# Neighbourhood attention: key columns in storage order for the scores, and a bias table with the row offset inside each block of key columns

## The chip, the cores and the metric

The kernel runs on one core of one Trainium2 chip. The metric is the device time of one execution in microseconds; a kernel's time is the median over its runs. The profile is one execution taken by the hardware profiler. Engines are named as the profile names them: PE (TensorE matmuls), PEld (TensorE weight loads, which overlap PE), DVE (VectorE), ACT (ScalarE), POOL (GpSimd) and SP (SyncE, whose queue issues nearly all DMAs).

## The reference

A trunk of two layers over 1024 tokens of width 1024. Each layer is a token mixer and a squared-ReLU MLP of width 4096, each with a pre-RMSNorm and a residual add; a last RMSNorm closes it. The mixer of the first layer is the neighbourhood attention that the change touches, that of the second a gated DeltaNet.

The tokens form a grid of 16 rows and 64 columns. In the attention each of 16 heads of width 64 lets a query see 8 rows and 16 columns of keys around it, with a learned bias per head, row offset and column offset:

```
s = einsum('bhrd,bhkd->bhrk', q, k) * scale + bias     # bias from rpb[h, drow, dcol]
p = softmax(where(mask, s, -inf))                      # mask: 8 rows x 16 columns around the query
o = p @ v;   out = (o reshaped) @ w_o
```

Everything is float32.

## The kernel before

Each large product is made of three passes in a reduced float format (F32R): every operand is split into a high and a low part, and hi x hi, hi x lo and lo x hi are added up in PSUM. Weights come by DMA in pieces of 256 KB (`wraw`, three buffers, line 97), ACT makes the high part (line 108) and DVE the low part (line 109), and `product` (line 120) runs the matmuls at line 132.

Tokens are kept in the order (column block of 8, row, column inside the block). So one tile of 128 tokens is one block of 8 grid columns with all its 16 rows, there are 8 such tiles, and a query tile needs the keys of its own block and of the blocks beside it: three key tiles (384 keys), or two (256) for the first and the last.

`load_x` (line 312) loads and transposes x and computes the values v for all heads; its second half of the columns uses four late weight loads (`wvraw`, line 320). `na` (line 403) then goes through 8 pairs of heads, n = 0 to 7. For each pair it computes k and q with `product`, splits them, and copies halves between partitions with DMAs from POOL's queue (lines 440 and 447). Then for each query tile t and each of the two heads:

- two score matmuls (line 468): q against the keys of two or three tiles, first hi x hi over 64 rows, then both cross products at once over 128 rows. The moving operand `kv` is a view of the keys with the row outermost: row, block, column. It is read in runs of 8 elements, and the scores lie in PSUM in the order (row, block, column);
- DVE (line 471) adds the bias, negates, and takes the extreme over the keys in the same instruction;
- ACT (line 474) takes the exponential and its sum. It reads and writes through the same permuting view, so that the result `e` lies in the order (block, row, column) of the keys as they are stored;
- DVE divides by the sum (lines 478 and 479), PE transposes 128 keys at a time (line 482), ACT or DVE copies the result (lines 485 and 487), and PE multiplies by v (line 492).

The bias comes from a table in DRAM, `natab` [head, query column, row offset, 56 key columns]. The 56 key columns are three sets: 24 for inner query tiles, 16 for the first and 16 for the last. `na_bias_table` builds it on DVE and writes it with 16 DMAs (line 307). `load_bias` (line 413) brings a pair's bias into SBUF with 32 DMAs (line 418), one for each head and grid row. Four tiles `bias0` to `bias3` hold two pairs; they share memory with the low weight parts of the values, so POOL clears them (line 410) only after the values' products. All DMAs of lines 97, 307, 320 and 418 stand in SP's queue.

The order in which the engines get their instructions in this stage is not the order of the code: the framework schedules them when the kernel is built. In the trace the k and q products of the next pair are mixed into the attention of the current one. The order of the DeltaNet stage is written out with a planner of its own (`Meter`, `Jobs`), which this stage does not use.

Of the kernel before, what the change touches and what calls it, by code (L numbers as in the profile page):

```python
# [8 lines left out]
FP32 = mybir.dt.float32  # L9
F32R = mybir.dt.float32r  # L10
AF = mybir.ActivationFunctionType
# [4 lines left out]
P = 128  # L16
# [7 lines left out]
# the share of the tensor engine's array to be kept at work, and the quanta kept for the inverses  # L24
AC = 0.47
RS = 9
# quanta of dense jobs by the end of the gates, and of the preparation of the first head
G1 = 49
G2 = 75
# how long before a chain is ready its next step is emitted, and the slack in which epilogues are  # L30
SL = 0.45
DV = 1.2
# quanta of dense jobs by the end of each head's period, and in its first part
# [4 lines left out]
class Trunk:  # L38
# [45 lines left out]
    # gain vector as one column per feature tile  # L84
# [5 lines left out]
    # weight tile: rows of src x 128 columns -> (hi, lo) of each 128 rows  # L90
# [21 lines left out]
    # 4 KB per partition, one of two sets of 16  # L112
# [6 lines left out]
    # psum[128 columns, half of the tokens] = w^T x  # L119
# [16 lines left out]
    # the halves of the last feature tiles are interleaved, so that the first half of the tokens is done early  # L136
# [4 lines left out]
    # one half of a feature tile of the next normalised input: hi, lo of gain * h, and the running sum of squares  # L141
# [24 lines left out]
    # r = 1/sqrt(sum / D + EPS)  # L166
# [5 lines left out]
    # one column per token tile  # L172
# [11 lines left out]
    # the same factors, tokens along the free dimension  # L184
# [12 lines left out]
    # the last product of all is cut in two with cut, so that what follows the first part starts earlier  # L197
# [93 lines left out]
    # ---------------------------------------------------------------- neighbourhood attention  # L291
    NEG = -1.0e30

    def na_bias_table(self, rpb):
        """DRAM table [head, query column, row offset, 24 + 16 + 16 key columns], masked by columns."""
        nc = self.nc
        tab = self.dram.tile([16, 8, 15, 56], FP32, name="natab")
        for g in range(2):
            src = self.work("rpb", [120, 31], 2)
            nc.sync.dma_start(out=src, in_=rpb[8 * g:8 * g + 8].rearrange("h r c -> (h r) c"))  # L300
            e = self.half("r")[:120, 0:448].rearrange("p (q k) -> p q k", k=56)
            nc.vector.memset(e, self.NEG)
            for qc in range(8):
                for dst, idx in ((qc, 7), (24, 15 - qc), (40, 7 - qc)):
                    nc.vector.tensor_copy(out=e[:, qc, dst:dst + 16], in_=src[:, idx:idx + 16])
            for h in range(8):
                nc.sync.dma_start(out=tab[8 * g + h].rearrange("q r k -> r q k"), in_=e[15 * h:15 * h + 15])
        return tab

    # x -> transposed residual stream, tokens in order (column block of 8, row, column); and the values,  # L310
    # tokens on partitions, the first of them feature tile by feature tile while x is transposed
    def load_x(self, gain, wqkv):
# [39 lines left out]
        for half in range(2):  # L352
            sl = slice(half * HALF, (half + 1) * HALF)
            for d in range(ND):
# [7 lines left out]
                # squares of a token tile's half, with their sums per token  # L362
# [40 lines left out]
    def na(self, st, v, wqkv, rpb):  # L403
# [4 lines left out]
        for i in range(4):  # L408
            b = self.work(f"bias{i}", [P, 16, 56])
            nc.gpsimd.memset(b, self.NEG)  # L410
            bias.append(b)

        def load_bias(n):
            for hh in range(2):
                for r in range(16):
                    r0 = min(max(r - 4, 0), 8)
                    d0 = 7 + r0 - r
                    nc.sync.dma_start(out=bias[n % 2 * 2 + hh][r * 8:r * 8 + 8, r0:r0 + 8, :], in_=tab[2 * n + hh, :, d0:d0 + 8, :])
# [3 lines left out]
        for n in range(8):  # L422
            # q and k of two heads A, B, split: the two cross products of hi and lo in one pass over 128 rows,
            # rows of q A: hi, lo; q B: lo, hi; k A: lo, hi; k B: hi, lo
# [30 lines left out]
            for t4 in range(2):  # L455
                ops = self.bank("o", [P, HALF], 2)
                for t in range(4 * t4, 4 * t4 + 4):
# [3 lines left out]
                    c0 = 24 if t == 0 else (40 if t == 7 else 0)  # L461
                    pts = []
                    for hh in range(2):
                        pr = slice(64 * hh, 64 * hh + 64)
                        sps = self.bank("pa", [P, HALF])
                        for i, (qt, kt) in enumerate(((qs[hh][pr], khi[pr]), (qs[hh], ks[hh]))):
                            kv = kt[:, b0 * P:b1 * P].rearrange("p (b r c) -> p r b c", b=nb, c=8)
                            nc.tensor.matmul(out=sps[:, :w], lhsT=qt[:, t * P:(t + 1) * P], rhs=kv, start=i == 0, stop=i == 1)
# [3 lines left out]
                                                       in1=bias[n % 2 * 2 + hh][:, :, c0:c0 + 8 * nb],  # L472
                                                       op0=ALU.add, op1=ALU.min, scale=-1.0, scalar=3.0e38, accum_out=nm)
                        nc.scalar.activation(out=e[:, :w].rearrange("p (b r c) -> p r b c", b=nb, c=8),
                                             in_=s[:, :w].rearrange("p (r b c) -> p r b c", b=nb, c=8),
                                             func=AF.Exp, scale=-1.0, bias=nm, accum_out=sm)
# [57 lines left out]
    # ---------------------------------------------------------------- gated DeltaNet  # L534
    # Heads of width 128, chunks of 128 tokens.  q', k', v are silu(conv) without l2 norms, which per-token
    # factors carry:
    #   c = |k'|^2 + EPS,  s = beta / c,  vs = v sqrt(c),  vn = s * X (vs - e^G k'S),
    #   X = (I + N diag(s))^-1,  N = causal part of (k' k'^T) * decay,  S <- e^Glast S + (k' e^(Glast-G))^T vn
    # The backward direction is the same with the masks transposed and the chunks taken from the last.
# [15 lines left out]
    def gdn_gates(self, st, w, a_log, dt):  # L555
        """beta, decay rates and their sums inside a chunk: [token, direction, chunk, head]."""
# [7 lines left out]
        # four groups of 32 output partitions at once, added up when transposed  # L564
# [33 lines left out]
        # softplus: max(x, 0) + log(1 + e), e = exp(-|x|); the rounding of 1 + e is added back  # L598
# [18 lines left out]
        # sums of g: up to a token, after it, over the chunk  # L617
# [9 lines left out]
    # The chains below (preparation, inverses, scan, output) are latency-bound; they are generators that  # L627
    # yield where a step waits for another engine, and quanta of dense jobs are emitted there.

    def conv_job(self, jobs, st, w, cw, out, ready=lambda: True, done=lambda: None):  # L630
        """out = silu(conv(projection)), channels on partitions."""
# [74 lines left out]
    def gdn_decay(self, h, hd):  # L706
        """Squared norms and decays within a chunk."""
# [3 lines left out]
        # decay between tokens of a chunk, transposed: E[j, i] = exp(sum of g between them)  # L711
# [33 lines left out]
        # squared norms of k', q' per token  # L745
# [24 lines left out]
    def gdn_prep(self, h, hd):  # L770
        """Products within a chunk, and the inverses of the 32-wide diagonal blocks."""
# [14 lines left out]
        def scale(b2, ps):  # L786
            # L = N^T rows scaled by s; E <- (q' k'^T * decay)^T
# [16 lines left out]
        # diagonal blocks -> one problem per partition (direction, chunk, block); both lower triangular  # L804
# [7 lines left out]
        # forward elimination, even columns of the inverse on partitions 0-63, odd ones on 64-127  # L812
# [26 lines left out]
    def gdn_levels(self, hd, arrive=lambda: None):  # L839
        """Full inverses Y[j, i] = X[i, j] of a chunk, blocks of 32 -> 64 -> 128.  # L840
        Forward: rows of the first half feed the second; backward: the other way round."""
# [64 lines left out]
    # the blocks' inverses go to DRAM when the elimination is about done, which other transfers need not wait for  # L906
# [5 lines left out]
    # out = scale * in, on the engine that is free first  # L912
# [15 lines left out]
    # squares of a chunk and their sums per token, on the engine that is free first  # L928
# [7 lines left out]
    # scaled values, tokens on partitions  # L936
# [15 lines left out]
    def gdn_scan(self, h, hd):  # L952
# [10 lines left out]
        def outputs():  # L963
            # this step's contributions to the output, emitted behind the next step's first products
# [65 lines left out]
    def gdn_out(self, h, hd, onorm):  # L1030
        nc, o = self.nc, hd["o"]
        # gated norm: o / sqrt(|o|^2 / 128 + 128 EPS |q'|^2)
# [23 lines left out]
    def gdn_body(self, st, first, w, a_log, dt, wo):  # L1056
# [46 lines left out]
        for h in range(8):  # L1103
            end = EN[h]
            jobs.until(lambda: "vt" in heads[h])
            # the next head is prepared as soon as the tiles and banks of the other chains are free
# [37 lines left out]
    # half of the output of an earlier head, back from DRAM, in place of the projections' input  # L1144
# [11 lines left out]
    def wo_jobs(self, jobs, wo, ys):  # L1156
        """Output projection of the first heads, added to the residual in DRAM."""
# [39 lines left out]
class Meter:  # L1197
    """Passes instructions on and estimates when the engines will be through with them (in us)."""
# [25 lines left out]
    # when what a chain waits for is there: a tile to be written, a buffer to be free, a time  # L1224
# [11 lines left out]
    # share of the tensor engine's array that was at work in the last 3.4 us, which its clock depends on  # L1236
# [65 lines left out]
class Jobs:  # L1302
    """Dense jobs, emitted in quanta of one 128-row product (three passes) and of one op of their epilogues."""
# [113 lines left out]
    def mix(self, chains, end, rest=[], fill=True):  # L1417
        """Emit the chains, each when what its next products wait for is about there, and quanta of the jobs,
        up to their number end, while there is nothing to emit of the chains. Chains added meanwhile may be left."""
# [96 lines left out]
```

## Time and profile before

| | |
|---|---|
| median of 3 runs | 2853.98 us (2852.11 to 2857.23) |
| span of the profiled execution | 2853.0 us; no other time of it is given |
| PE busy | 2782.4 us, 98% |
| DVE, ACT, POOL busy | 1377.4, 938.7, 604.7 us |
| granted TensorE clock | 0.994 |
| score matmuls, line 468 | 256, from 137.8 to 518 us |
| bias DMAs, line 418 | 256 of 14.0 KB |
| table DMAs, line 307 | 16 of 26.2 KB |

The busy time of PE counts each matmul from its start to a modelled end, and matmuls overlap, so the time that a matmul really takes from the engine is read from start to start. `128*128` in a row of the profile is the shape of the array that a matmul uses (rows * columns), and `128x384` the shape of its output.

### The profile page before, as it was taken

How to read it: one execution, taken by the hardware profiler on the slowest of the kernel's cores; microseconds unless marked ns; L12 is line 12 of the kernel's file. 1: busy time of each engine (PE TensorE's matmuls, PEld its weight loads, DVE VectorE, ACT ScalarE, POOL GpSimd, SP SyncE). 2: the span in 40 equal slices, each digit the busy share in tenths (PEclk: the TensorE clock that was granted, in tenths of full speed). 3: DMA queues.
4: the chain of work that ended last, by engine and by line, in shares of the span. 5: the costliest groups of instructions: out<-in, count | busy, mean ns of one | idle time of the engine just before them, and what ended most of it. 6: DMA issues, size and time to landing. Idle time of an engine off the chain costs nothing. (4 is left out here: it accounts for less than half of the span.)

```text
span 2853.0 us, 39344 instructions
## 1 busy us (share of the span) xinstructions
PE 2782.4 (98%) x14844; PEld 2198.5 (77%) x14844; DVE 1377.4 (48%) x2905; ACT 938.7 (33%) x2111; POOL 604.7 (21%) x871
## 2 busy tenths in 40 slices
PE   8999999999999999999998999899989999999998
PEld 6766666788888888877777878787868888888887
DVE  5155556433232232334767888887563232232333
ACT  5144444332121121223445555455342121121134
POOL 0101111121010010112155545543142011020111
PEclk9999999999999999999999999999999999999999
DMA  7212212221111111123112222114331111111123
GB/s 194 53 44 58 52 45 51 96 60 49 48 45 51 45 48 49 45 71 91 43 41 51 53 53 50 43 43 117 114 117 50 45 48 49 45 49 48 45 70 115
DMA packets 308588, 177.13 MB, mean 62 GB/s; under 512 B 75054, under 2 KB 286638, under 8 KB 308398
## 3 DMA queue, kind: packets, MB, share of 16 engines
q1 hardware_dynamic: 299982, 166.13, 20.6%
q0 software_dynamic: 3072, 8.39, 1.3%
q8 instruction: 117, 1.92, 0.3%
q10 hardware_dynamic: 5344, 0.09, 0.1%
q14 instruction: 73, 0.60, 0.1%
HBM read 141.62 MB, written 24.55 MB: 58 GB/s over the span
## 5 line engine op out<-in xcount | busy, mean ns | idle before, releaser
L132 PE MATMUL mm<-X,whi 128*128 128x512 f32 x2800 | 902.2, 400 | 0.9 <-ACT X L499 0.7
L132 PE MATMUL mm<-A,whi 128*128 128x512 f32 (+1 forms) x2124 | 669.9, 396 | 3.3 <-ACT whi L108 1.9
L132 PEld LDWEIGHTS mm<-X,whi 128*128 128x128 f32 x2800 | 525.3, 188 | 132.2 <-issue 7.5
L132 PE MATMUL mm<-X,wlo 128*128 128x512 f32 x1400 | 559.7, 400 | 0.0
L132 PEld LDWEIGHTS mm<-A,whi 128*128 128x128 f32 x2124 | 398.9, 189 | 100.0 <-ACT whi L108 2.9
L108 ACT CAST whi<-wraw 128x512 fp32r<-128x512 f32 (+1 forms) x338 | 208.0, 616 | 792.6 <-PE mm L132 760.1
L132 PE MATMUL mm<-A,wlo 128*128 128x512 f32 (+1 forms) x1062 | 419.8, 396 | 2.5 <-DVE wlo L109 2.5
L1189 PE MATMUL mm<-A,whi 128*128 128x512 f32 x1216 | 404.5, 413 | 1.1 <-DVE A L1189 1.1
L223 POOL TENSOR_TENSOR r<-r 128x512 f32<-128x512 f32 x128 | 152.1, 1188 | 1104.6 <-DVE r L221 1098.5
L109 DVE TENSOR_TENSOR wlo<-wraw,whi 128x512 fp32r<-128x512 f32 (+1 forms) x338 | 243.3, 721 | 199.0 <-ACT whi L108 198.6
L132 PEld LDWEIGHTS mm<-X,wlo 128*128 128x128 f32 x1400 | 263.8, 188 | 63.0 <-issue 1.7
L1189 PEld LDWEIGHTS mm<-A,whi 128*128 128x128 f32 x1216 | 214.8, 191 | 41.4 <-DVE A L1189 1.9
L1189 PE MATMUL mm<-A,wlo 128*128 128x512 f32 x608 | 241.6, 397 | 0.0
L132 PEld LDWEIGHTS mm<-A,wlo 128*128 128x128 f32 x1062 | 200.6, 189 | 50.3 <-DVE wlo L109 3.4
L221 DVE SCALAR_TENSOR_TENSOR r<-mm,rs 128x512 f32<-128x512 f32 x128 | 88.5, 691 | 287.7 <-PE mm L132 286.8
L250 DVE TENSOR_TENSOR h<-mm,h 128x512 f32<-128x512 f32 x111 | 76.7, 691 | 300.4 <-PE mm L132 300.4
L1189 POOL TENSOR_TENSOR xt<-lp,xi 128x126 f32<-128x126 f32 (+22 forms) x248 | 110.4, 445 | 174.5 <-DMA lp<-dsc 155.7
L1189 DVE SCALAR_TENSOR_TENSOR X<-xp,cw,X 128x512 f32<-128x512 f32 x192 | 141.9, 780 | 1.7 <-ACT X L1189 1.0
L1189 PEld LDWEIGHTS mm<-A,wlo 128*128 128x128 f32 x608 | 115.3, 190 | 28.0
L164 POOL TENSOR_TENSOR rs<-rs,r 128x512 f32<-128x512 f32 x55 | 75.7, 1381 | 269.0 <-ACT r L163 268.7
L1189 POOL TENSOR_TENSOR xi<-xi,xt 128x126 f32<-128x126 f32 (+22 forms) x248 | 112.6, 454 | 19.4
L222 ACT ACTIVATE X<-r 128x512 fp32r<-128x512 f32 x64 | 40.6, 634 | 170.6 <-DVE r L221 170.6
(264 smaller groups left out, 3148.7 us busy)
## 6 DMA issues: line engine op xcount, KB each, us to landing
wraw<-in_mlp_w_dram SPq DMA_DIRECT2D x276, 256.0 KB
wraw<-in_gdn_w_in_dram SPq DMA_DIRECT2D x64, 256.0 KB
wraw<-in_na_w_qkv_dram SPq DMA_DIRECT2D x32, 256.0 KB
h<-hs SPq DMA_DIRECT2D x16, 512.0 KB
wraw<-in_na_w_o_dram SPq DMA_DIRECT2D x20, 256.0 KB
A<-in_x_dram SPq DMA_DIRECT2D x16, 256.0 KB
wvraw<-in_na_w_qkv_dram SPq DMA_DIRECT2D x8, 512.0 KB
hs<-A SPq DMA_DIRECT2D x16, 256.0 KB
```

The lines of the kernel that those rows point to most:

```text
L108: nc.scalar.copy(out=hi[:, :nk], in_=raw[:, :nk])
L109: nc.vector.tensor_tensor(out=lo[:, :nk], in0=raw[:, :nk], in1=hi[:, :nk].bitcast(FP32), op=ALU.subtract)
L132: nc.tensor.matmul(out=ps, lhsT=a, rhs=b, start=n == 0, stop=n == last)
L164: nc.gpsimd.tensor_tensor(out=st["acc", half], in0=st["acc", half], in1=sq, op=ALU.add)
L221: nc.vector.scalar_tensor_tensor(out=r, in0=ps, scalar=0.0, in1=st["rstd", half], op0=ALU.max, op1=ALU.mult)
L222: nc.scalar.activation(out=ahi[:, sl], in_=r, func=AF.Square)
L223: nc.gpsimd.tensor_tensor(out=q, in0=r, in1=r, op=ALU.mult)
L250: nc.vector.tensor_tensor(out=hv, in0=ps, in1=hv, op=ALU.add)
L1189: r = f(*args, **kw)
```

## The change

The keys are read as they are stored, blocks outermost, so the scores come out in the order (block, row, column). The bias must lie in the same order, so the table becomes [head, query column, block of 8 key columns, row offset, 8 columns], with 7 blocks in place of 56 columns, and the bias tile [128, 7 blocks, 16 rows, 8 columns]. The exponential has nothing left to permute. The number of matmuls, of elements and of DMAs is the same. A bias DMA now moves, for each of 8 query columns, 7 runs of 64 elements in place of one run of 448; a table DMA moves 15 x 56 runs of 8 elements in place of 15 x 8 runs of 56.

Comments and docstrings are also blanked all over the file; those parts are left out here.

```diff
     def na_bias_table(self, rpb):
...
-        tab = self.dram.tile([16, 8, 15, 56], FP32, name="natab")
+        tab = self.dram.tile([16, 8, 7, 15, 8], FP32, name="natab")
...
             for h in range(8):
-                nc.sync.dma_start(out=tab[8 * g + h].rearrange("q r k -> r q k"), in_=e[15 * h:15 * h + 15])
+                nc.sync.dma_start(out=tab[8 * g + h].rearrange("q b r c -> r (q b) c"), in_=e[15 * h:15 * h + 15].rearrange("r q (b c) -> r (q b) c", c=8))
...
-            b = self.work(f"bias{i}", [P, 16, 56])
+            b = self.work(f"bias{i}", [P, 7, 16, 8])
...
-                    nc.sync.dma_start(out=bias[n % 2 * 2 + hh][r * 8:r * 8 + 8, r0:r0 + 8, :], in_=tab[2 * n + hh, :, d0:d0 + 8, :])
+                    nc.sync.dma_start(out=bias[n % 2 * 2 + hh][r * 8:r * 8 + 8, :, r0:r0 + 8, :], in_=tab[2 * n + hh, :, :, d0:d0 + 8, :])
...
-                    c0 = 24 if t == 0 else (40 if t == 7 else 0)
+                    c0 = 3 if t == 0 else (5 if t == 7 else 0)
...
-                            kv = kt[:, b0 * P:b1 * P].rearrange("p (b r c) -> p r b c", b=nb, c=8)
-                            nc.tensor.matmul(out=sps[:, :w], lhsT=qt[:, t * P:(t + 1) * P], rhs=kv, start=i == 0, stop=i == 1)
+                            nc.tensor.matmul(out=sps[:, :w], lhsT=qt[:, t * P:(t + 1) * P], rhs=kt[:, b0 * P:b1 * P], start=i == 0, stop=i == 1)
...
                         nc.vector.tensor_tensor_reduce(out=s[:, :w], in0=sps[:, :w],
-                                                       in1=bias[n % 2 * 2 + hh][:, :, c0:c0 + 8 * nb],
+                                                       in1=bias[n % 2 * 2 + hh][:, c0:c0 + nb].rearrange("p b r c -> p (b r c)"),
                                                        op0=ALU.add, op1=ALU.min, scale=-1.0, scalar=3.0e38, accum_out=nm)
-                        nc.scalar.activation(out=e[:, :w].rearrange("p (b r c) -> p r b c", b=nb, c=8),
-                                             in_=s[:, :w].rearrange("p (r b c) -> p r b c", b=nb, c=8),
-                                             func=AF.Exp, scale=-1.0, bias=nm, accum_out=sm)
+                        nc.scalar.activation(out=e[:, :w], in_=s[:, :w], func=AF.Exp, scale=-1.0, bias=nm, accum_out=sm)
```

## The prediction

> **What bounds the kernel now.** I read the page first, then the table by stages, then the groups by shape of the attention stage, then single matmuls in the timeline.
>
> ```profile
> span 2853.0 us, 39344 instructions
> ...
> PE 2782.4 (98%) x14844; PEld 2198.5 (77%) x14844; DVE 1377.4 (48%) x2905; ACT 938.7 (33%) x2111; POOL 604.7 (21%) x871
> ```
>
> TensorE is busy for 98% of the span. The change touches only the neighbourhood attention, so what counts is whether that stage has the same limit. It runs up to 526 us; in its middle one head pair takes 49.4 us. Two stretches of the stage table, the second full head pair and the last one:
>
> ```profile
> 190.00:239.40 49.40, 49.40 (x261) 33.08 (x260) 29.35 (x87) 21.16 (x53) 6.82 (x10) 1.00 0.22 54
> ...
> 486.00:526.30 40.30, 38.17 (x214) 24.45 (x212) 29.57 (x86) 21.35 (x52) 1.46 (x3) 1.00 0.33 106
> ```
>
> The columns are the stretch, its length, then busy time and instructions of TensorE, its weight loads, VectorE, ScalarE and GpSimd, then the granted clock, the DMA share and GB/s. In a full head pair TensorE has no idle time at full clock, VectorE works 29.35 us of the 49.40, ScalarE 21.16, and DMA is at 22%. Only the last pair, which has no later products to fill with, leaves 2.1 us idle. So a microsecond taken from VectorE or ScalarE is worth nothing before that end, and a microsecond taken from TensorE is worth a microsecond. The question is what the permuted reading costs TensorE. Here is what the groups by shape seem to say:
>
> ```profile
> L132 PE MATMUL mm<-X,whi 128*128 128x512 f32 x482 | 168.5, 411 | 0.9 <-ACT X L499 0.7 <-DVE X L500 0.2
> ...
> L474 ACT ACTIVATE e<-r,nm 128x384 f32<-128x384 f32 x96 | 59.2, 617 | 23.5 <-ACT e L474 11.8 <-DVE nm L471 10.4 <-issue 1.2
> ...
> L468 PE MATMUL pa<-wvraw,qk 128*128 128x384 f32 x96 | 42.9, 447 | 0.0
> ...
> L474 ACT ACTIVATE e<-r,nm 128x256 f32<-128x256 f32 x32 | 16.1, 506 | 7.7 <-DVE nm L471 7.6
> ```
>
> A score matmul that reads 384 permuted columns is given 447 ns, a product that reads 512 columns in order 411 ns. That looks like a heavy price for the permutation. But matmuls overlap, so I take the distance from one start to the next instead.
>
> **TensorE: the permuted reading against reading in order.** Timeline of TensorE in three places; the columns are start, length, engine, line, operation:
>
> ```profile
> 247.98 0.38 PE L492 MATMUL o<-r,A 128*64 128x128 f32 x2
> 248.29 0.50 PE L132 MATMUL mm<-X,whi 128*128 128x512 f32 x1
> 248.72 0.44 PE L468 MATMUL pa<-qk,qk 64*128 64x384 f32 x1
> 249.09 0.45 PE L468 MATMUL pa<-wvraw,qk 128*128 128x384 f32 x1
> ...
> 250.40 0.45 PE L468 MATMUL pa<-wvraw,qk 128*128 128x384 f32 x1
> 250.69 0.39 PE L132 MATMUL mm<-X,whi 128*128 128x512 f32 x1
> 251.01 0.43 PE L492 MATMUL o<-r,A 128*64 128x128 f32 x2
> ```
>
> ```profile
> 217.59 0.39 PE L468 MATMUL pa<-qk,qk 64*128 64x256 f32 x1
> 217.91 0.39 PE L468 MATMUL pa<-wvraw,qk 128*128 128x256 f32 x1
> 218.14 0.39 PE L132 MATMUL mm<-X,wlo 128*128 128x512 f32 x1
> ```
>
> ```profile
> 2839.36 0.39 PE L132 MATMUL mm<-A,whi 128*128 128x256 f32 x2
> 2839.59 0.28 PE L132 MATMUL mm<-A,wlo 128*128 128x256 f32 x1
> 2839.70 0.28 PE L267 MATMUL pa<-ones,rs 128*128 128x1 f32 x2
> ```
>
> And two stretches of the first MLP; the second is its last block, where line 242 reads the moving operand in 8 x 8 runs of 8 elements:
>
> ```profile
> 1130.00:1230.00 100.00, 100.00 (x430) 80.58 (x429) 33.75 (x50) 20.07 (x32) 16.76 (x14) 1.00 0.16 48
> 1236.00:1332.00 96.00, 96.00 (x386) 72.70 (x385) 35.93 (x52) 31.77 (x51) 18.57 (x14) 1.00 0.31 96
> ```
>
> Reading in order, back to back: 512 columns take 100.00 / 430 = 0.233 us, 256 columns (2839.36 to 2839.70, three of them) 0.113 us, so 384 lie at 0.173. Around a change of tile shape (the 128*128, 64*128, 128*64 in the rows) there is more. The product at 250.69 has a change behind it and takes 0.32 to the next start: 0.09 more than 0.233. The product at 248.29 has a change on both sides and takes 0.43: another 0.11. So one change costs 0.20 us, and no permutation was involved in either row.
>
> Now the score matmuls. The one with 128 rows has a change ahead of it: in order it should take 0.173 + 0.11 = 0.283, the row (250.40 to 250.69) has 0.29. The one with 64 rows has a change on both sides: 0.173 + 0.20 = 0.373, the row (248.72 to 249.09) has 0.37. With 256 columns 0.223 against 0.23 (217.91 to 218.14) and 0.313 against 0.32 (217.59 to 217.91). The differences are +7, -3, +7 and +7 ns, on rows rounded to 10 ns. So nearly all that sets 447 ns apart from a cheap matmul is the change of tile shape, and that stays. There are 96 matmuls of each 384 kind and 32 of each 256 kind: 96 x 0.007 - 96 x 0.003 + 64 x 0.007 = 0.8 us. Bounds: below, nothing. Above, the MLP stretches: 96.00 / 386 - 0.233 = 0.016 us for 64 runs of 8, or 0.25 ns a run; 48 runs in 384 columns and 32 in 256 give 192 x 12 + 64 x 8 ns = 2.8 us. I take 0.8, since those rows are of the matmuls in question.
>
> **ScalarE and VectorE.** The exponential (line 474) now reads and writes in order. A ScalarE operation over 256 elements, in order and with a sum, is this one (groups by shape, first stage):
>
> ```profile
> L372 ACT ACTIVATE r<-A 128x256 f32<-128x256 f32 x16 | 6.5, 408 | 1.2 <-DVE sums L369 1.1
> ```
>
> It is another function, but by it the 506 ns could fall by 0.1 us; over 128 of them 13 us at most, all of it under a saturated TensorE. The reduction of line 471 reads the same number of elements; I take nothing off it. What is left is the end of the last pair, where TensorE waits for the softmax of the last tiles, two exponentials one behind the other: 0.2 us gained, bounds 0 and 0.6 (the last three tiles).
>
> **DMA.** The number of DMAs is unchanged; their runs get shorter. Writing the table (line 307): 16 DMAs of 15 x 8 runs of 224 bytes become 15 x 56 runs of 32 bytes, 840 instead of 120 packets each. Loading the bias (line 418): 256 DMAs of 8 runs of 1792 bytes become 56 runs of 256 bytes. Both go through SyncE's queue, in this order, with weights behind them:
>
> ```profile
> 50.10 0.81 SPq L307 DMA_DIRECT2D natab<-r  x2
> ...
> 53.98 5.37 SPq L307 DMA_DIRECT2D natab<-r  x8
> 66.67 1.80 SPq L320 DMA_DIRECT2D wvraw<-in_na_w_qkv_dram  x2
> 68.53 2.78 SPq L307 DMA_DIRECT2D natab<-r  x6
> 71.35 2.49 SPq L97 DMA_DIRECT2D wraw<-in_na_w_qkv_dram  x3
> 112.18 21.75 SPq L418 DMA_DIRECT2D bias<-natab  x64
> ```
>
> ```profile
> 221.09 10.84 SPq L418 DMA_DIRECT2D bias<-natab  x32
> 232.02 22.68 SPq L97 DMA_DIRECT2D wraw<-in_na_w_qkv_dram  x4
> ```
>
> What a packet costs I read from the DMA view of three stretches. Packets, MB and share of 16 engines: 50 to 66.6 us (ahead of the loads at 66.67); 1497 to 1501 us (1024 of the packets are writes of 128 bytes to DRAM); 600 to 700 us (nearly only packets of 512 bytes):
>
> ```profile
> q1 hardware_dynamic: 1782, 1.06, 22.1%
> ```
>
> ```profile
> q1 hardware_dynamic: 1185, 0.15, 23.9%
> ```
>
> ```profile
> q1 hardware_dynamic: 9771, 4.85, 16.8%
> ```
>
> The second gives 0.239 x 4 us x 16 / 1185 = 12.9 ns a packet, the third 0.168 x 100 us x 16 / 9771 = 27.5 ns. Ten table DMAs stand ahead of the loads at 66.67: 8400 packets x 12.9 ns / 16 = 6.8 us of all engines. From 50 to 66.6 us the engines are free for 77.9% of 16.6 us = 12.9 us. So the table is out before the loads begin, and it delays nothing up to 12.9 us x 16 / 8400 = 24.6 ns a packet. These loads do matter: TensorE stops for their second half already, between 74.12 and 75.28 us.
>
> ```profile
> 74.12 0.86 PE L347 MATMUL mm<-qk,X 128*128 128x512 f32 x3
> 75.28 0.50 PE L347 MATMUL mm<-bias,X 128*128 128x512 f32 x1 [0.29 <-DVE bias L329]
> ...
> 123.64 0.62 ACT L108 CAST whi<-wraw 128x512 fp32r<-128x512 f32 x1 [1.17 <-PE mm L132]
> ...
> 252.62 0.60 ACT L108 CAST whi<-wraw 128x512 fp32r<-128x512 f32 x1
> ```
>
> The six table DMAs behind (4.1 us) delay only the weights issued at 71.35, whose first use is no earlier than the cast at 123.64, and the bias load that waits until 112.18 for other reasons. For the bias loads the price lies between 12.9 and 27.5 ns a packet: 32 x 56 packets a head pair, 1.4 to 3.1 us of all engines within the 10.84 us in which they are issued. Their issue itself takes 10.84 / 32 = 0.34 us each now; the table's DMAs, with 120 packets, take 2.78 / 6 = 0.46. So SyncE's queue is held between 0 and 32 x 0.12 = 4 us longer a head pair. Behind it stand the weights of the next pair, issued at 232.02 and cast at 252.62: over 15 us of cover remain. The bias itself, loaded at 221 to 232, serves the pair that starts at 289. If that cover were gone, 4 us a pair would come straight onto TensorE.
>
> The Trainium skill speaks against these shorter runs: "DMA: Bandwidth & Descriptors", section Specifications, gives 512 bytes as the least transfer for line rate and says that below it a read-modify-write happens. The row of 128-byte writes shows no such price, at 12.9 ns against 27.5 for four times the bytes; by the rule the 32-byte writes could cost more, which is the third rival.
>
> **Sum.** The profiled execution spans 2853.0 us; no time of its own is given beside the span, and the median of the runs, 2853.98, is 0.98 above it, which I carry along. 2853.0 - 0.8 - 0.2 + 0.98 = **2853.0 us**, within 2850.6 (both upper bounds) and 2854.0 (no gain). A measurement of this kernel tells about 0.2%, 5.7 us, from no change, so my forecast is no measurable change: 0.60.
>
> **Rival 1: the instructions come in another order.** In the code the products of the next head pair stand behind this pair's attention; in the timeline they are mixed into it (248.29, 250.69). So the framework orders the engines' streams when the kernel is built, and access patterns and DMA shapes that cost differently in its reckoning can reorder them. Each change of tile shape costs 0.20 us, and I count 59 in the 261 matmul records of the stretch from 190 to 239.4. Four more or fewer in each of eight pairs are 6.4 us: 2846.6 or 2859.4. For it: much is mixed by small margins. Against it: no dependency and no number of operations changes, and TensorE's stream waits for no DMA in a full pair. 0.22 (0.08 faster, 0.06 within 0.2%, 0.08 slower).
>
> **Rival 2: the permuted reading costs what the groups show.** By durations, 256 in-order columns take 280 ns (2839.59) and 512 take 411, so 384 would take 345 and not 447: about 0.1 us x 256 = 26 us, 2827. The Trainium skill, "Advanced Engine Details and Errata", section PSUM Cachelines, says that any non-contiguous access pattern slows matmuls significantly, though of PSUM, and here the pattern is in SBUF. Against it stand the four start-to-start comparisons and 16 ns in the MLP. 0.08.
>
> **Rival 3, slower: the 32-byte writes hold the queue.** Up to 24.6 ns a packet nothing happens; beyond, each ns delays the loads at 66.67 by 8400 / 16 = 0.53 us, and TensorE, which has no slack there, by as much. At four times the 128-byte price, 52 ns, that is 14 us: 2867. It is measurable from 24.6 + 5.7 / 0.53 = 36 ns. For it: no row shows a write of under 128 bytes in number. Against it: 12.9 ns, falling with size. 0.10.
>
> **How the numbers follow.** Faster by over 0.2%: 0.08 + 0.08 = 0.16. Within: 0.60 + 0.06 = 0.66. Slower: 0.08 + 0.10 = 0.18. The range is the likeliest case widened by rival 1, 2846.6 to 2859.4; left out are rivals 2 and 3, 0.18, and a little of 1.
>
> **What would show it.** Right: line 468 keeps about 440 ns in the groups and 0.28 and 0.37 us from start to start with 384 columns; a full head pair still takes 49.2 to 49.4 us; the exponential falls to about 0.5 us without effect; the loads at 66.67 move by under 1 us. Wrong: a head pair of 46 us (rival 2), another count of shape changes a pair (rival 1), or TensorE idle near 75 us for over 5 us (rival 3).

## The result, and the profile after

The changed kernel takes 2964.62 us (median of 4 runs, 2950.16 to 2965.21); the kernel before took 2855.61 us beside it. The ratio is 1.037 with an interval of 1.035 to 1.039: slower by 3.7%, far outside the predicted range. The profiled execution took 2950.16 us, some 14 us less than the median, with a span of 2948.4 us and a mean granted clock of 0.966 (before: 2853.0 us and 0.994).

The page of the kernel after; the last line is the granted TensorE clock in 40 slices of the span, in tenths:

```profile
span 2948.4 us, 39257 instructions
...
PE 2844.1 (96%) x14844; PEld 2244.9 (76%) x14844; DVE 1378.5 (47%) x2905; ACT 938.3 (32%) x2111; POOL 604.7 (21%) x871
...
PEclk9988878799999999999999999999999999999999
```

As many matmuls as before, but the clock falls in the slices of the neighbourhood attention, and nowhere else. The first weight of the MLP behind the attention is issued at 690.3 us where it was 592.7, so the whole loss of the spans, 95.4 us, lies ahead of it. The table by stages of the kernel after, with the columns of the prediction (the granted clock is the last but two); three head pairs, from one bias load to the next, and then, from the third of them, the part without products:

```profile
239.28:301.36 62.08, 57.09 (x253) 39.19 (x252) 27.53 (x86) 19.10 (x50) 6.86 (x10) 0.81 0.19 42
301.36:364.42 63.06, 58.08 (x270) 39.66 (x271) 28.18 (x86) 20.99 (x54) 6.87 (x10) 0.84 0.19 41
364.42:433.45 69.03, 64.46 (x263) 43.78 (x262) 29.40 (x87) 21.64 (x54) 6.78 (x10) 0.73 0.16 38
...
385.00:426.00 41.00, 38.48 (x139) 23.52 (x138) 18.09 (x69) 13.67 (x37) 1.03 (x2) 0.55 0.12 30
```

These pairs take 62 to 69 us in place of 49.4, with about the same number of matmuls. Length times clock is 50.3, 53.0 and 50.4 us: a pair, in microseconds at full clock and with its idle time, is nearly what it was. What is new is the clock.

Where it falls shows in the timeline of TensorE in the same pair:

```profile
385.84 0.39 PE L132 MATMUL mm<-X,wlo 128*128 128x512 f32 x1
386.16 0.38 PE L467 MATMUL pa<-qk,qk 64*128 64x256 f32 x1
...
387.54 0.44 PE L467 MATMUL pa<-qk,qk 64*128 64x384 f32 x1
387.91 0.44 PE L467 MATMUL pa<-wvraw,qk 128*128 128x384 f32 x1
389.71 0.69 PE L467 MATMUL pa<-qk,qk 64*128 64x384 f32 x1 [1.37 <-DVE nm L470]
...
397.68 0.69 PE L467 MATMUL pa<-qk,qk 64*128 64x384 f32 x1
398.30 0.69 PE L467 MATMUL pa<-wvraw,qk 128*128 128x384 f32 x1
398.92 0.69 PE L489 MATMUL o<-r,A 128*64 128x128 f32 x2
```

At 385.84 the last product (line 132) starts; then come the scores (line 467, 468 before) of all tiles with no product between them. At first the two scores with 384 columns lie 0.37 us apart, as before. After a wait of 1.37 us for DVE they lie 0.62 apart, and so until the next products. TensorE is not waiting there: it is busy 38.48 of 41.00 us, at a clock of 0.55.

The instructions stand in another order, then. In the program as built, these are the runs of successive products (line 132) between the first score and the last multiplication by v:

```
          number of runs   runs of more than 12 products
before    164              50, 49, 50, 50, 50, 50, 50
after      28              34, 48, 96, 92, 96, 96, 96, 96
```

Before, half of a pair's 96 products stood in one run and half were mixed singly into the attention; now all 96 stand together and the attention is alone. On SyncE's queue the loads have changed places with the weights as well (timeline of SyncE, after; the rows of before are in the prediction):

```profile
54.62 6.08 SPq L307 DMA_DIRECT2D natab<-r  x8
67.28 1.80 SPq L320 DMA_DIRECT2D wvraw<-in_na_w_qkv_dram  x2
69.13 5.74 SPq L307 DMA_DIRECT2D natab<-r  x6
...
231.97 1.69 SPq L418 DMA_DIRECT2D bias<-natab  x2
238.84 0.38 SPq L97 DMA_DIRECT2D wraw<-in_na_w_qkv_dram  x1
239.28 20.80 SPq L418 DMA_DIRECT2D bias<-natab  x30
260.19 1.64 SPq L97 DMA_DIRECT2D wraw<-in_na_w_qkv_dram  x3
```

One bias load is now issued in 20.80 / 30 = 0.69 us (0.34 before). The table's DMAs take 0.76 and 0.96 us each, and the loads behind them at 67.28 come 0.6 us later than before, in a trace whose first table DMA is already 1.1 us later (51.22 against 50.10). TensorE's stop there is much the same as before, 1.20 us between the two starts (1.16 before):

```profile
74.71 0.89 PE L347 MATMUL mm<-qk,X 128*128 128x512 f32 x3
75.91 0.50 PE L347 MATMUL mm<-bias,X 128*128 128x512 f32 x1 [0.30 <-DVE bias L329]
```

### The profile page after: what moved, and what is told of

Same layout as the page of the kernel before. It is cut to its first block, busy times and chain, and to the rows that moved or that the text cites. A ratio compares the mean times of both kernels' runs of the same rounds, so it can differ in the third digit from the quotient of the medians.

```text
span 2948.4 us, 39257 instructions
## 1 busy us (share of the span) xinstructions
PE 2844.1 (96%) x14844; PEld 2244.9 (76%) x14844; DVE 1378.5 (47%) x2905; ACT 938.3 (32%) x2111; POOL 604.7 (21%) x871
## 5 line engine op out<-in xcount | busy, mean ns | idle before, releaser
L132 PE MATMUL mm<-X,whi 128*128 128x512 f32 x2800 | 889.8, 399 | 5.7 <-ACT whi L108 4.8
L489 PE MATMUL o<-r,A 128*64 128x128 f32 x704 | 101.0, 346 | 15.1 <-DVE r L484 9.4
```

Source lines behind the costliest of these rows:

```text
L132: nc.tensor.matmul(out=ps, lhsT=a, rhs=b, start=n == 0, stop=n == last)
L489: nc.tensor.matmul(out=ops[64 * hh:64 * hh + 64, (t % 4) * P:(t % 4 + 1) * P], lhsT=v[b0 + j][:, c:c + 64], rhs=pts[hh][:, j * P:(j + 1) * P],
```

## The experiments

Theory A: the new shape of the bias DMAs makes the framework put the instructions in another order, products in blocks, and this order makes the time by itself. Rivals: the DMAs hold something up while the kernel runs; reading in order costs or brings something; the waits of the bare attention on the softmax, rather than the clock, set the time.

**The DMAs alone.** The new table, bias tile and loads; keys and exponential are permuted as before, and DVE reads the new tile through a view of the old shape, so the bias values are the wrong ones.

```diff
-  kt[:, b0 * P:b1 * P]                                            # as in the changed kernel
+  kt[:, b0 * P:b1 * P].rearrange("p (b r c) -> p r b c", b=nb, c=8)
...
-  nc.scalar.activation(out=e[:, :w], in_=s[:, :w], ...)
+  nc.scalar.activation(out=e[:, :w].rearrange("p (b r c) -> p r b c", b=nb, c=8), in_=..., ...)
```

> Table, bias tile and bias DMAs as in the changed kernel; keys and exponential read through the permuting views as before. The bias lands in another order than it is read in, so the scores get wrong bias values; the instructions, their sizes and waits are those of the real thing. The built order of all engines is the changed kernel's: 96 products of a pair in one block, then its attention. Theory A (the short runs of the bias DMAs make the scheduler separate products and attention): ratio 1.035 to 1.040, 2955 to 2968 us. Theory B (reading in order is what costs): ratio 1.00.

2960.59 us, ratio 1.039 (1.035 to 1.042), span 2950.4, clock 0.965. As built, the order on TensorE, SyncE and VectorE is exactly that of the changed kernel. The whole loss comes with the DMAs and their tiles.

**The reading alone, in three cuts.** All reading edits on the old table; then the keys and the exponential without DVE's view; then DVE's view by itself.

```diff
-  rhs=kt[:, b0 * P:b1 * P].rearrange("p (b r c) -> p r b c", b=nb, c=8)
+  rhs=kt[:, b0 * P:b1 * P]
...
-  in1=bias[n % 2 * 2 + hh][:, :, c0:c0 + 8 * nb]
+  in1=bias[n % 2 * 2 + hh].rearrange("p r k -> p (r k)")[:, c0 * P // 8:c0 * P // 8 + w]
...
-  nc.scalar.activation(out=e[:, :w].rearrange(...), in_=s[:, :w].rearrange(...), ...)
+  nc.scalar.activation(out=e[:, :w], in_=s[:, :w], ...)
```

> Keys, bias and exponential read in order; table and DMAs as before (so the bias values are read from other places than they were written to, and the scores are wrong; instructions and sizes are those of the real thing). The built order mixes products and attention as before, with small differences in the first pairs. Theory A and the prediction's sum: 2852 to 2856 us, ratio 0.998 to 1.001. Theory B: ratio 1.03 or more.

> The kernel before with the keys read in storage order and the exponential without its permuting view; bias, table, DMAs and DVE's reading as before, so the bias meets the wrong columns and the values of the scores are not those of the reference. As built, the order on every engine is that of the kernel before. By the prediction's own step this is worth 0.8 us of TensorE and 0.2 us at the end: ratio 0.9990 to 1.0003, span 2849 to 2855. If the +0.27% of reading_alone came from reading in order itself, this kernel shows it too: 1.002 to 1.003. If the permutation cost the durations of the groups (rival 2), 0.990 to 0.992.

> The kernel before with nothing but DVE's view of the bias changed: it reads the same number of elements of the bias tile as one flat run (of the wrong columns, so the scores are not those of the reference). As built, only this edit of the reading edits moves instructions: the products of the first pairs stand in other places. If the +0.27% of reading_alone comes from that order, this kernel shows it alone: ratio 1.001 to 1.004, and the weights of the MLP are first issued 4 to 8 us later than the 592.7 us of before. If not: 0.9995 to 1.0005.

All reading edits: 2860.13 us, 1.0027 (1.0017 to 1.0037), more than its expectation allowed. Keys and exponential: 2854.71 us, 1.0006 (0.9997 to 1.0015), no difference. DVE's view alone: 2862.19 us, 1.0028 (1.0017 to 1.0040). So the little loss of the reading edits comes with one of them. It goes with a change of order too: DVE's reduction takes no longer (544 ns with 384 columns, 543 before), but with the flat view as built the second run of products is 70 long (before: 49), and the stretch from one bias load to the next is this one, of the kernel with DVE's view alone (stages):

```profile
166.47:219.38 52.91, 50.22 (x243) 33.00 (x242) 28.41 (x87) 20.96 (x53) 6.83 (x10) 0.87 0.25 59
```

Its clock is 0.87, in a stretch that had 1.00 before. TensorE's timeline of the kernel with keys and exponential in order:

```profile
247.47 0.44 PE L468 MATMUL pa<-qk,qk 64*128 64x384 f32 x1
247.84 0.44 PE L468 MATMUL pa<-wvraw,qk 128*128 128x384 f32 x1
248.12 0.49 PE L482 MATMUL pt<-ident,e 128*128 128x128 f32 x3
```

0.37 us behind the 64-row score and 0.28 behind the other, against 0.37 and 0.29 in the prediction's rows: a permuted operand costs TensorE next to nothing here. The exponential (groups by shape, the same kernel) isn't quicker either:

```profile
L474 ACT ACTIVATE e<-r,nm 128x384 f32<-128x384 f32 x96 | 59.2, 617 | 22.0 <-PE pt L482 10.6 <-DVE nm L471 8.8 <-DVE e L479 1.7
```

617 ns against 617 with 384 columns, and 507 against 506 with 256.

**The order alone.** The kernel before, its DMAs untouched; the products of a pair are only queued behind the last matmul of the pair ahead.

```diff
-  ps = self.product(w, x, half)
+  with self.tc.issue_after(last) if n else nullcontext():      # last: the pair's last matmul of line 492
+      ps = self.product(w, x, half)
```

> The kernel before, DMAs and reading unchanged; only each pair's products are queued on TensorE behind the attention of the pair ahead, so that they stand in one block of 96 as in the changed kernel. Theory A: ratio 1.025 to 1.045, 2925 to 2983 us, with the granted clock at 0.5 in parts of the attention. Theory C (SyncE's queue, held 21 us a pair by the longer bias issues, brings the weights late, and the order matters little): ratio 1.000 to 1.005.

2968.55 us, 1.041 (1.039 to 1.042), clock 0.955. A pair, from one bias load to the next (stages):

```profile
243.19:309.95 66.76, 63.28 (x262) 42.82 (x260) 28.08 (x87) 21.07 (x52) 6.87 (x10) 0.73 0.16 39
```

With the cheap bias loads of before, the block order alone gives the loss.

**The same expensive queue, the order mixed.** The kernel before, every bias DMA cut in two.

```diff
-  nc.sync.dma_start(out=bias[..][r * 8:r * 8 + 8, r0:r0 + 8, :], in_=tab[2 * n + hh, :, d0:d0 + 8, :])
+  for j in range(0, 8, 4):
+      nc.sync.dma_start(out=bias[..][r * 8:r * 8 + 8, r0 + j:r0 + j + 4, :], in_=tab[2 * n + hh, :, d0 + j:d0 + j + 4, :])
```

> The kernel before (old table, old bias tile, permuted reading) with every bias DMA cut in two of 4 grid rows: 64 DMAs a pair of 8 runs of 896 bytes, no 32-byte or 256-byte runs anywhere. As built, the products stand in blocks in the first pairs (84 and 74 in a row) and mixed as before from the fourth pair on (longest run 50). Theory A (what SP's queue spends on bias DMAs makes the order, and the order makes the time): 2875 to 2915, ratio 1.008 to 1.021, with head pairs of 60 us or more first and of about 49.4 us later. Theory 'short runs in DRAM or SBUF cost the time': no loss, 0.999 to 1.002.

2889.31 us, 1.013 (1.011 to 1.014). As built, the products stand in runs of 84 and 74 first and of 50 from the fourth pair on. Stages and SyncE's queue of this kernel:

```profile
172.44:235.78 63.34, 56.56 (x223) 36.76 (x220) 28.92 (x89) 20.21 (x52) 6.69 (x10) 0.66 0.16 37
235.78:300.30 64.52, 61.07 (x262) 41.15 (x260) 28.26 (x84) 21.26 (x53) 6.86 (x10) 0.81 0.21 53
355.19:404.65 49.46, 49.46 (x261) 33.19 (x260) 28.46 (x87) 20.65 (x53) 6.81 (x10) 1.00 0.23 53
```

```profile
355.19 22.82 SPq L419 DMA_DIRECT2D bias<-natab  x64
378.10 24.56 SPq L97 DMA_DIRECT2D wraw<-in_na_w_qkv_dram  x4
```

This run separates the two. In the later pairs the bias holds SyncE's queue for 22.82 us, as in the changed kernel, weights behind it, and the pair takes 49.46 us: the cover of the prediction holds. The two pairs in blocks cost 28.8 us more than the same two before (49.76 and 49.33), most of the 35.6 lost in all. And no run as short as 256 bytes is needed: runs of 896 bytes, in twice as many DMAs, turn the order too.

**Fewer, later, elsewhere.** The changed kernel with 16 bias DMAs a pair, both heads using the first one's bias; with each pair's loads placed one pair later in the code; with the loads on GpSimd's queue.

```diff
+  if hh == 0:
       nc.sync.dma_start(out=bias[n % 2 * 2 + hh]..., in_=tab[2 * n + hh, ...])
---
+  load_bias(1)                                                    # ahead of the first pair
...
-  if n < 7:
-      load_bias(n + 1)
+  if n > 1:
+      load_bias(n)
---
-  nc.sync.dma_start(out=bias..., in_=tab...)
+  nc.gpsimd.dma_start(out=bias..., in_=tab...)
```

> The changed kernel with only the first head's bias loaded in each pair, 16 DMAs of 0.65 us in place of 32; the second head is computed with the first one's bias, so it is wrong. The built order mixes products and attention again as before. The table is still written in 32-byte runs. Theory A and theory C: 2850 to 2858 us. If the 32-byte writes of the table or the 256-byte runs as such were the cause, the time stays above 2900.

> The changed kernel with each pair's bias loaded one pair later in program order, behind its own weights; same number and shape of DMAs, SyncE held as long. The built order mixes products and attention partly: 66 products in a block and 30 mixed in, 132 runs of products in place of 28 (164 before). Theory A (the order decides): in between, 2860 to 2920 us. Theory C (the time that SyncE is held decides): 2940 us or more.

> The changed kernel with the bias DMAs issued from GpSimd's queue; shape and number unchanged. The built order mixes products and attention as before (166 runs of products). Theory A: 2845 to 2875 us, unless GpSimd, now with 32 more issues a pair ahead of its copies between partitions, delays the scores, then up to 2900. If the 256-byte runs themselves are the cause, 2940 or more.

With half the loads: 2854.69 us, 1.0005 (0.9996 to 1.0014); 164 runs of products as before. SyncE's timeline and a pair in the table by stages:

```profile
270.80 11.08 SPq L419 DMA_DIRECT2D bias<-natab  x16
```

```profile
270.80:320.16 49.36, 49.36 (x262) 33.18 (x260) 28.26 (x87) 20.57 (x53) 6.93 (x11) 1.00 0.20 48
```

The new tile, half of the short runs, the 32-byte writes and reading in order are all in it, and it costs nothing: 16 x 0.69 us is what 32 loads took before. Later loads: 2904.21 us, 1.017 (1.015 to 1.020), runs of 66 products, a pair of 56.86 us (stages):

```profile
304.80:361.66 56.86, 54.54 (x261) 36.44 (x260) 27.28 (x87) 20.49 (x54) 6.76 (x10) 0.89 0.20 46
```

GpSimd's queue: 2880.71 us, 1.009 (1.006 to 1.011), 166 runs. The order is mixed again; what is left has two places, an inner stretch and the last pair (stages):

```profile
360.00:410.00 50.00, 48.06 (x258) 32.70 (x259) 27.33 (x83) 20.05 (x51) 21.96 (x37) 1.00 0.22 51
510.00:560.00 50.00, 48.16 (x191) 30.85 (x191) 22.88 (x77) 17.80 (x47) 0.00 (x0) 0.62 0.24 90
```

TensorE idles about 2 us of 50 in the inner stretch, and the last pair, which has no products beside it for 27 us (508.6 to 535.6), runs at a clock of 0.62.

**The clock or the waits.** The changed kernel with three dummy matmuls, and with one, of 512 columns ahead of each transpose group, into the tile that the transposes overwrite.

```diff
   for hh in range(2):
...
+      for _ in range(3):                                          # or range(1)
+          nc.tensor.matmul(out=tps, lhsT=qs[hh][:, t * P:(t + 1) * P], rhs=ks[hh][:, 0:HALF], start=True, stop=True)
       for j in range(nb):
           nc.tensor.transpose(...)
```

> The changed kernel with three matmuls more for each head and query tile, ahead of the transposes, into the bank that the transposes overwrite: 384 matmuls of 128x128 by 512 columns, 90 us of TensorE work at full clock. Products and attention stay in blocks. If the halved clock of the attention blocks comes from TensorE's low activity in them, the dummies keep it up and the time hardly rises or falls: 2920 to 2990 us, granted clock above 0.985. If the clock falls for another reason, or the blocks are slow because of waits and not of the clock: 3040 us or more.

> The changed kernel with one dummy 512-column matmul of full array shape ahead of each transpose group (128 in all, 0.233 us each by the MLP's rate, 30 us of TensorE work), into the PSUM tile that the transposes then overwrite. The blocks of products stay. Theory 'the halved clock is a good part of the price of the blocks': if this little keeps the clock up (mean over 0.98), the kernel is faster than the changed one in spite of its extra work: ratio 1.020 to 1.036. Theory 'the waits on the softmax chain set the time of the blocks, and the clock only follows': 1.036 to 1.042 with the clock up. If one dummy does not hold the clock, its mean stays under 0.975 and nothing is told apart.

Three: 2964.42 us, 1.038 (1.037 to 1.040), clock 0.989. One: 2977.09 us, 1.043 (1.042 to 1.045), clock 0.968. One doesn't hold the clock, so the comparison that its expectation names is not to be had; but the two stand beside each other. Four pairs with three dummies, then two pairs with one (stages):

```profile
247.52:305.45 57.93, 57.32 (x283) 39.79 (x282) 27.79 (x80) 19.30 (x48) 6.78 (x10) 1.00 0.19 45
305.45:371.66 66.21, 63.94 (x302) 43.15 (x300) 29.46 (x85) 20.34 (x51) 6.86 (x10) 0.92 0.19 43
371.66:431.97 60.31, 59.58 (x296) 41.16 (x296) 28.55 (x83) 19.40 (x48) 6.86 (x10) 1.00 0.19 43
431.97:498.42 66.45, 65.75 (x324) 44.56 (x322) 31.81 (x91) 22.55 (x56) 6.77 (x10) 0.95 0.19 44
```

```profile
245.50:310.25 64.75, 62.65 (x268) 41.77 (x266) 28.93 (x86) 19.54 (x50) 6.77 (x10) 0.82 0.17 40
310.25:380.00 69.75, 66.78 (x287) 43.88 (x286) 30.25 (x87) 21.35 (x54) 6.86 (x10) 0.80 0.17 37
```

Three dummies don't hold the clock in every pair either, and they move the order as well: by the trace the blocks are 83 to 89 products long from the fourth pair on, and in the third stretch above TensorE is never without products for more than 13 us. So the pairs are not quite alike. Alike is the first whole attention without a product in it, from the last product ahead of it to the next one; here it is in the changed kernel, with one dummy and with three (stages of the three kernels):

```profile
196.63:238.14 41.51, 36.26 (x167) 22.17 (x165) 20.10 (x76) 16.49 (x46) 1.03 (x2) 0.71 0.11 28
```

```profile
198.81:244.36 45.55, 42.02 (x182) 24.77 (x180) 21.65 (x76) 16.91 (x46) 1.03 (x2) 0.74 0.09 26
```

```profile
204.55:246.38 41.83, 38.99 (x215) 24.45 (x213) 21.66 (x76) 16.87 (x46) 1.03 (x2) 1.00 0.11 27
```

With 32 dummies more than the second, at 0.233 us each 7.5 us of work, the third is 3.7 us shorter, and its clock is 1.00. Against the changed kernel its 48 dummies, 11.2 us of work, cost 0.3 us; by the medians all 384 (some 90 us) are free. And length times clock of the four pairs, less the 11.2 us of their dummies, is 46.7, 49.7, 49.1 and 51.9 us, about the 49.4 of before. So the waits on the softmax do not set the 62 to 69 us: an attention with more work in it is shorter when the clock is up.

**The price of a change of tile shape.** The kernel before; the hi x hi score matmul reads 128 rows, half of them zeros of q in two free tiles (not for the second head of the last two pairs, where no tile is free).

```diff
+  qz = [self.slot(f"A{7 - i}", F32R) for i in range(2)]            # zeros in the other head's rows
...
+  if i == 0 or n < 6:
+      nc.gpsimd.tensor_copy(out=qz[i][ab[i], sl], in_=qs[i][ab[i], sl])
...
-  ((qs[hh][pr], khi[pr]), (qs[hh], ks[hh]))
+  ((qz[hh], khi) if hh == 0 or n < 6 else (qs[hh][pr], khi[pr]), (qs[hh], ks[hh]))
```

> The kernel before; only the first score matmul runs over 128 rows in place of 64, with q's high part padded by zeros (for both heads in pairs 0 to 5, for one in 6 and 7), 4 more copies a pair on GpSimd. No tile shape changes between the score matmuls any more. By the prediction's price, 0.20 us a change and one to two changes less for 112 score pairs: 22 to 44 us faster, 2810 to 2832 us, ratio 0.985 to 0.992. If a change of tile shape costs nothing by itself: ratio 1.00.

2832.05 us, 0.992 (0.990 to 0.993): 23 us faster than the kernel before, at the low end of what was expected, and the fastest of all here. Two pairs of it, and its scores in the groups by shape:

```profile
211.20:257.08 45.88, 44.27 (x261) 32.80 (x259) 27.56 (x87) 20.43 (x53) 10.30 (x14) 1.00 0.22 57
257.08:304.88 47.80, 45.93 (x261) 34.23 (x260) 28.79 (x87) 20.19 (x53) 10.10 (x14) 0.96 0.22 54
```

```profile
L473 PE MATMUL pa<-wvraw,qk 128*128 128x384 f32 x96 | 35.4, 369 | 0.0
```

The changes of shape in the records of a pair fall from 58 to 29, and in the first of these pairs TensorE is busy 5.1 us less (49.40 to 44.27): 0.18 us a change, beside the prediction's 0.20. 1.6 us of it come back as idle time, and in the second pair the clock gives some more of it back, at 0.96. A score matmul that is still permuted is now given 369 ns; it was the neighbour of another shape, not the permutation, that stood in the 447.

## Why the prediction was wrong

Span, mean granted clock, and their product for the profiled executions (the clock is rounded to 0.001, some 3 us of the product):

| kernel | span, us | clock | product, us |
|---|---|---|---|
| before | 2853.0 | 0.994 | 2836 |
| after | 2948.4 | 0.966 | 2848 |
| DMAs alone | 2950.4 | 0.965 | 2847 |
| DVE's view alone | 2859.2 | 0.992 | 2836 |
| order alone | 2966.6 | 0.955 | 2833 |
| more DMAs | 2887.3 | 0.983 | 2838 |
| later loads | 2896.6 | 0.981 | 2842 |

The product hardly moves: of the 95 us some 83 are lost to the clock; some 12 are left in the product, as idle time or as work, and it does not tell which.

By the prediction's own steps:

- **The permuted reading** (0.8 us, bounds 0 and 2.8): right. Keys and exponential in order make no difference that can be measured. Rival 2, by which the durations count, is out.
- **ScalarE** (the exponential to fall by about 0.1 us): wrong, with 617 and 507 ns it takes the same time, so no run shows the 0.2 us that the sum takes off for the end of the last pair. Its size hardly matters to the sum.
- **VectorE**: nothing was taken off the reduction, and rightly so (543 ns with 384 columns, before and after). But its view was not free of effect: it moved the products of the first pairs, 0.28%.
- **The table's writes** (delay nothing up to 24.6 ns a packet; rival 3 above that): right. DMA view of the kernel after, 66 to 76 us; nearly all packets are under 512 bytes, most of them the table's writes of 32:

```profile
DMA packets 5468, 1.20 MB, mean 120 GB/s; under 512 B 4956, under 2 KB 4956, under 8 KB 5468
...
q1 hardware_dynamic: 5468, 1.20, 62.0%
```

  62.0% of 16 engines for 10 us are at most 99.2 / 5468 = 18 ns a packet, with the larger ones in it. Rival 3 is out.
- **The issue of the bias loads** (at most 0.12 us more each, 4 us a pair): mis-sized. From one issue to the next it is 0.69 us against 0.34, 11 us more a pair. I had read the price from the last six of the table's DMAs, which have more packets but took 0.46. The cover of over 15 us held all the same: more_dmas pays the full price for nothing in its later pairs.
- **Rival 1** is what happened, and its working is the step that failed. Its mechanism was right: shapes that cost differently reorder the streams. Its price wasn't: "Four more or fewer in each of eight pairs are 6.4 us" takes it that only single instructions change places. The runs showed that whole blocks do, and that this order alone costs 4.1% (2968.55 us), nearly all of it as clock. And its argument against, "no dependency and no number of operations changes, and TensorE's stream waits for no DMA in a full pair", speaks of the time of running; the order is made at build time. What I did not ask is what holds the products in between the scores, and what the attention costs without them. The prediction took the last pair for an answer: it "has no later products to fill with" and shows only 2.1 us idle. That was a misreading. The table by stages for line 132 alone, the same stretch of the kernel before and then the bare attention of the kernel after:

```profile
486.00:526.30 40.30, 14.97 (x50) 8.46 (x48) 1.00 0.33 106
```

```profile
385.00:426.00 41.00, 1.23 (x6) 0.67 (x4) 0.55 0.12 30
```

There were 50 products in the last pair too. The longest stretch of the kernel before without one lies at its end (timeline of TensorE):

```profile
516.28 0.39 PE L132 MATMUL mm<-X,wlo 128*128 128x512 f32 x1
...
525.60 0.50 PE L132 MATMUL mm<-X,whi 128*128 128x512 f32 x1 [0.68 <-ACT X L499]
```

Those 9.3 us ran at a clock of 1.00; the kernel after has stretches of 38 to 47 us, and in the one shown above the matmuls are slow from 389.71 on, 3.9 us behind the start of the last product. So no row of before showed a whole attention without products, and the short piece that it showed did not give the price away.

The chance that I gave to "slower" by this way was 0.08, and at 6.4 us, a fifteenth of the 95.4 us of the spans. In the sum itself the order stands at nothing; that is the term that was missing.

What isn't settled: by which rule the framework turns longer bias loads into blocks. The runs show only which edits turn the order (the loads' issue on SyncE's queue doubled, by shape or by number; a little, DVE's view) and which turn it back (half as many, another queue; one pair later, in part). Why more_dmas is mixed again from the fourth pair on, at the same load, isn't explained. Nor was a block order run at full clock without added work, so its price at full clock is only estimated, by the product column and by the pairs with three dummies. And why the clock falls within 4 us in one stretch without products and not in the 9.3 us of another is open.

## What to carry to other kernels

Where a framework orders the instructions, a change of a DMA's shape is a change of the order until the built order shows otherwise: compare the built streams first, then price the operations. A TensorE stage at full clock can owe its clock to what is mixed into it, as here; ask what it runs at without that, and multiply the span by the granted clock to tell lost clock from lost work. And before blaming an access pattern, take start-to-start distances and count the changes of tile shape, which here cost more than the pattern.

## What the runs showed of the hardware

- **The clock falls without a long stall.** In the 41 us of bare attention TensorE is busy 38.48 us and its longest wait is 1.37 us; the granted clock is 0.55. With sixteen matmuls of 512 columns more a pair it is 0.82 and 0.80 in the two pairs shown, with 48 between 0.92 and 1.00 in four. The Trainium skill, "TensorE: Matmul & The Clock Gate", section "HAM oscillation — how this bites in real kernels", gives as its rule to leave no TensorE gap of over some 3.4 us. No wait of that length is in this stretch and the clock fell all the same; what the gate counts there no run here shows.
- **Issuing a DMA of few, short runs can cost more than one of many.** From one issue to the next on SyncE's queue, 56 runs of 256 bytes took 0.69 us, 120 runs of 224 bytes 0.46 (the last six table DMAs of before), 8 runs of 1792 bytes 0.34. Neither bytes nor runs alone order these.
- **A change of tile shape on TensorE costs about 0.18 to 0.20 us** by these traces, and zeros in place of a 64-row matmul were cheaper here than the change (2832.05 against 2855.50 us). The Trainium skill, "TensorEngine Tiling (Array Packing)", section "Key Properties", says that changing the tiling mode drains TensorE; this case adds its size.
